# Input projection of a hybrid layer: weights stationary, 512 tokens a row, seven products for eight, and head data through DRAM

## The chip, the cores and the metric

One NeuronCore of a Trainium2 chip runs the whole layer. The metric is the device time of one launch in microseconds; three timed runs of the kernel before gave 1645.48, 1645.70 and 1645.99 (median 1645.7). Engines are named as the profile names them: PE (TensorE), PEld (its weight loads), DVE (VectorE), ACT (ScalarE), POOL (GpSimd), and SP, whose queue issues most DMAs.

## The reference, cut to what matters

The layer takes 1024 latent tokens and 256 context tokens of width 1024. It normalises and modulates them, and multiplies them with one wide matrix:

```
IN_WIDTHS = (512, 512, 512, 512, 512, 512, 512, 512, 16, 1024, 1024)
rq, rk, rv, rg, mq, mk, mv, mo, mg, bg_ret, bg_ml = (h @ w for w in jnp.split(w_in, offsets, axis=-1))
rq = apply_rope(to_heads(rq, 4), cos, sin); rk = apply_rope(to_heads(rk, 4) * 128 ** -0.5, cos, sin)
ret_x = retention(rq, rk, rv) forward + backward, chunks of 128, from the context's final state
ml_x = mlstm(mq, mk, mv, mg) forward + backward, in the same way
merged = sigmoid(bg_ret) * (y_ret @ w_ret_up) + sigmoid(bg_ml) * (y_ml @ w_ml_up)
x = x + g1 * (merged @ w_out)
x = x + g2 * swiglu(modulate(rms_norm(x)), w_ffn_in, w_ffn_out); out = rms_norm(x)
```

Four retention heads and four mLSTM heads of 128 columns each need keys, values, queries and an output gate (rg or mo). The context needs keys and values only. The queries and keys of retention are rotated by position: their two halves are mixed with cosines and sines. The 16 columns mg are the gates of the mLSTM. All is in float32.

## The kernel before, in words

**Products in parts.** A float32 operand is split into two float32r parts, hi (a rounded copy, made on ACT) and lo (the rest, made on DVE), and a product is three matmuls, hi x hi, hi x lo and lo x hi (`mm3`, L89 to L95). Weights come in by DMA as `raw`, 512 columns at a time, and are split into `whi` and `wlo` (`load_w_half`, L73 to L83).

**Projection.** Modulated tokens lie feature-major (`xh` for latents, `ch` for context). For a chunk of 128 tokens, `project` (L447) keeps a 128 x 128 piece of the tokens stationary and moves a row of 256 weight columns past it (272 with the gate columns, for the first block), 24 matmuls to one PSUM tile. `kv_tile` (L459) does this for the key and the value of a head for ten chunks, of which the first two are context; `qg_tile` (L470) for query and gate for eight. The result is token-major, as the scans want it; `rope` (L438) rotates it on DVE and POOL. The first four chunks are computed while the modulation is still being made (`first_tiles`, L348).

**Heads and scans.** Loop L787 goes through heads u = 1 to 7. After each chunk's tile it calls `tick` (L726), which advances what runs beside the projection by one slot: the scan of head u - 1 (`scan`, L481), the gate recurrence (`gates`, L626, under head 1), and the modulation of the later stages (`ada2`, L702, from head 2 on). The scan reads keys, values, queries and gates from SBUF; it transposes queries and keys on PE (`stage_a`, L536), forms scores (`stage_b`), outputs (`stage_c`), states (`decay` on POOL at L497, `advance` with PE at L511), and writes y to DRAM (`put_y`). The gate recurrence goes chunk by chunk: transposes, two scans of 128 per direction on DVE (L656, L658), and columns back by PE.

**Lift and merge.** Retention outputs are lifted with `w_ret_up` (`up_mm`, L808) and parked in DRAM. Then come the gate columns bg: eight blocks of 256 output columns by 1024 inputs. The first is computed plainly (`plain_block`, L239: 96 matmuls of 512 columns); seven are computed by Winograd's form (`winograd_block`, L249: seven products of 512 inputs x 128 columns x 512 tokens in place of eight, 84 matmuls). For that form `seven` (L203) builds seven weight factors from four quarters, and `factors_of_parts` (L872) four token factors `t1` to `t4`. Seven additions per block, on DVE, put the products together.

**Later stages.** Output projection with `mm3` (rows of 512), second norm, FFN (two plain blocks, then 20 blocks of seven products), FFN output and final norm.

**Order.** Each engine works through its instructions in a fixed order. That order is laid out when the kernel is built, by an estimate of readiness, and isn't the order of the text. Waits between engines are semaphores. PSUM has eight tiles of 512 columns: four `mm`, four `sc`.

## Time and profile before

| what | value |
|---|---|
| median of three runs | 1645.7 us |
| span of the profiled execution, first to last instruction | 1643.1 us |
| around the span, against the median | 2.6 us |
| PE busy | 1604.8 us, 98% |
| PEld busy | 1395.8 us, 85% |
| DVE busy | 1005.4 us, 61% |
| ACT busy | 631.2 us, 38% |
| POOL busy | 423.6 us, 26% |
| DMA | 199.13 MB, mean 121 GB/s |

The profile lists the span of its execution and no device time of its own; what lies around the span is therefore taken against the median. The head stage runs from about 130 to 600 us, lift and merge to about 866, the output projection and second norm to about 990, the FFN to 1360, its output to the end. A matmul's busy time overlaps its neighbours', so the pace of PE is read from the distance of starts in a timeline, not from the mean time of one.

### The profile page before, as it was taken

Reading aid. Unit: us, or ns where it says so; the run is one execution under the profiler, and the core shown is the slowest. Engines: PE = TensorE matmul, PEld = TensorE weight load, DVE = VectorE, ACT = ScalarE, POOL = GpSimd, SP = SyncE. Lnnn points to the kernel's source line nnn. Section 1 sums busy time; section 2 is a strip of 40 time slices with the busy share of each in tenths; the row PEclk is TensorE's granted clock in tenths of the full one; section 3 lists DMA queues with packets and bytes.
Section 4 is the critical chain, followed back from the end, with each engine's and each line's share of the span. In section 5 each row is a group of like instructions: output and inputs, shape, how many; then the busy total and the mean of one; then the engine's idle time right before and its main releaser. Section 6 shows DMA issues by size and latency. Waiting matters only on the chain.

```text
span 1643.1 us, 25962 instructions
## 1 busy us (share of the span) xinstructions
PE 1604.8 (98%) x9326; PEld 1395.8 (85%) x9326; DVE 1005.4 (61%) x2223; ACT 631.2 (38%) x1512; POOL 423.6 (26%) x593
## 2 busy tenths in 40 slices
PE   7998999999999999999999999999999999999997
PEld 2798999999999998888877777888888888887887
DVE  5768555644645445678875777667677666536233
ACT  4555332333435355443343453323333334423230
POOL 1546244332322422233330225111111111001001
PEclk9999999999999999999999999999999999999998
DMA  9211223332432244444457412222222224735531
GB/s 328 103 62 35 73 84 104 100 101 91 136 104 91 71 149 135 161 173 161 142 183 252 130 56 71 90 96 85 96 84 83 92 88 168 268 108 179 162 103 52
DMA packets 114033, 199.13 MB, mean 121 GB/s; under 512 B 13104, under 2 KB 24048, under 8 KB 113904
## 3 DMA queue, kind: packets, MB, share of 16 engines
q1 hardware_dynamic: 112032, 195.38, 36.1%
q10 hardware_dynamic: 1872, 2.10, 0.4%
q8 instruction: 73, 1.20, 0.3%
q14 instruction: 56, 0.46, 0.1%
HBM read 160.66 MB, written 36.77 MB: 120 GB/s over the span
## 4 chain that ended last, share of the span: by engine, by line
PE 79%; DVE 7%; POOL 5%; issue 5%; DMA 2%; ACT 1%; SPq 0%; DVEq 0%; POOLq 0%; ACTq 0%
PE mm L95 9%; PE mm L93 9%; PE mm L94 9%; PE mm L1127 5%; PE mm L1129 5%; PE sc L229 5%; PE sc L230 5%; PE sc L231 5%; PE mm L1128 5%; PE mm L229 5%; PE mm L231 5%; PE mm L230 5%; PE sc L511 2%; PE sc L328 1%; POOL hid L995 1%
## 5 line engine op out<-in xcount | busy, mean ns | idle before, releaser
L93 PE MATMUL mm<-whi,A 128*128 128x256 f32 (+1 forms) x992 | 289.8, 292 | 0.9 <-DVE gtok L468 0.9
L95 PE MATMUL mm<-whi,A 128*128 128x256 f32 (+1 forms) x992 | 281.7, 284 | 0.2 <-DVE A L316 0.2
L94 PE MATMUL mm<-wlo,A 128*128 128x256 f32 (+1 forms) x992 | 281.3, 284 | 0.0
L174 DVE TENSOR_TENSOR wlo<-raw,whi 128x512 fp32r<-128x512 f32 x178 | 132.1, 762 | 114.8 <-ACT whi L173 114.6
L93 PEld LDWEIGHTS mm<-whi,A 128*128 128x128 f32 x992 | 190.3, 192 | 1.4 <-DVE gtok L468 1.1
L173 ACT CAST whi<-raw 128x512 fp32r<-128x512 f32 x178 | 106.2, 619 | 221.6 <-PE mm L1128 79.8
L95 PEld LDWEIGHTS mm<-whi,A 128*128 128x128 f32 x992 | 190.2, 192 | 0.5 <-DVE A L316 0.4
L94 PEld LDWEIGHTS mm<-wlo,A 128*128 128x128 f32 x992 | 190.6, 192 | 0.0
L995 POOL TENSOR_TENSOR hid<-hid,sg 128x512 f32<-128x512 f32 x44 | 84.8, 1931 | 329.0 <-DVE hid L255 294.0
L229 PE MATMUL mm<-A,whi 128*128 128x512 f32 x320 | 124.7, 390 | 2.4 <-DVE sg L255 1.7
L230 PE MATMUL mm<-A,whi 128*128 128x512 f32 x320 | 125.2, 391 | 1.0 <-DVE A L316 1.0
L231 PE MATMUL mm<-A,wlo 128*128 128x512 f32 x320 | 125.0, 391 | 0.0
L82 DVE TENSOR_TENSOR wlo<-raw,whi 128x512 fp32r<-128x512 f32 (+1 forms) x112 | 76.4, 708 | 53.6 <-ACT whi L81 53.6
L173 ACT CAST whi<-stg 128x512 fp32r<-128x512 f32 x108 | 61.9, 618 | 106.7 <-PE sc L230 62.2
L81 ACT CAST whi<-raw 128x512 fp32r<-128x512 f32 (+1 forms) x112 | 65.3, 619 | 41.1 <-PE mm L94 13.9
L497 POOL TENSOR_SCALAR vs<-v,colq 128x129 f32<-128x129 f32 x72 | 48.0, 676 | 127.6 <-PE sc L511 127.6
L229 PE MATMUL sc<-A,whi 128*128 128x512 f32 x208 | 80.9, 389 | 0.0
L230 PE MATMUL sc<-A,whi 128*128 128x512 f32 x208 | 80.9, 389 | 0.0
L231 PE MATMUL sc<-A,wlo 128*128 128x512 f32 x208 | 80.9, 389 | 0.0
L174 DVE TENSOR_TENSOR wlo<-stg,whi 128x512 fp32r<-128x512 f32 x108 | 80.0, 779 | 0.7 <-ACT whi L173 0.7
L1127 PE MATMUL mm<-A,whi 128*128 128x512 f32 (+1 forms) x204 | 77.8, 382 | 0.0
L1129 PE MATMUL mm<-A,wlo 128*128 128x512 f32 (+1 forms) x204 | 77.8, 381 | 0.0
(350 smaller groups left out, 4057.1 us busy)
## 6 DMA issues: line engine op xcount, KB each, us to landing
raw<-wffn SPq DMA_DIRECT2D x88, 256.0 KB
raw<-wfo SPq DMA_DIRECT2D x88, 256.0 KB
raw<-wada SPq DMA_DIRECT2D x64, 256.0 KB
raw<-win SPq DMA_DIRECT2D x60, 256.0 KB
hid_d<-hid SPq DMA_DIRECT2D x44, 256.0 KB
hraw<-hid_d SPq DMA_DIRECT2D x40, 256.0 KB
araw<-wada SPq DMA_DIRECT2D x32, 256.0 KB
bc<-rows_d SPq DMA_DIRECT2D x64, 128.0 KB
```

What stands on the lines that cost most here:

```text
L93: nc.tensor.matmul(ps, lhsT=lh, rhs=rh, start=i == 0, stop=False)
L94: nc.tensor.matmul(ps, lhsT=lh, rhs=rl, start=False, stop=False)
L95: nc.tensor.matmul(ps, lhsT=ll, rhs=rh, start=False, stop=i == n - 1)
L173: nc.scalar.copy(hi, x)
L174: nc.vector.tensor_tensor(out=lo, in0=x, in1=hi.bitcast(F32), op=ALU.subtract)
L229: nc.tensor.matmul(ps, lhsT=w[0][:, c], rhs=x[0][:, k, :], start=start and k == 0, stop=False)
L230: nc.tensor.matmul(ps, lhsT=w[0][:, c], rhs=x[1][:, k, :], start=False, stop=False)
L231: nc.tensor.matmul(ps, lhsT=w[1][:, c], rhs=x[0][:, k, :], start=False, stop=stop and k == 3)
L995: nc.gpsimd.tensor_tensor(out=c, in0=c, in1=sgs[f, hf], op=ALU.mult)
L1127: nc.tensor.matmul(ps, lhsT=w[0][:, c], rhs=h[0][:, t], start=kt == 0, stop=False)
L1128: nc.tensor.matmul(ps, lhsT=w[0][:, c], rhs=h[1][:, t], start=False, stop=False)
L1129: nc.tensor.matmul(ps, lhsT=w[1][:, c], rhs=h[0][:, t], start=False, stop=kt == 2 * NG - 1)
```

## The change

- **Projection.** Weights are stationary, and rows of 512 tokens move. Output is feature-major: 128 columns of a head by 512 tokens. Head 0 is computed plainly; heads 1 to 7 by seven products, two blocks a head (key and value, query and gate), with the form that the gate blocks and the FFN have. The token factors t1 to t4 are built once, right after the second half of the latents is modulated, and serve the heads and all eight gate blocks.
- **The form itself.** `winograd_block` now lets four products of a block run on in one PSUM tile (`chain`) and two in another (`third`); ACT copies three intermediate states (`snap`) and the last result, DVE does three additions. `run_blocks` places a block's last two products behind the first of the next. The FFN uses it too. PSUM's four `mm` tiles are now two `ch` and two `ts`. One of the weight sums goes to POOL.
- **Context.** Keys and values of the context are 48 matmuls of 256 columns a head (`context_kv`). For heads 1 to 7 the context's parts are read back from DRAM (`context_stream`) for each head.
- **Head data.** Keys, values and gates are transposed to token-major on PE (`store_tokens`), queries and keys stay feature-major as well, and all are written to DRAM. `scan` of head u - 2 loads them back chunk by chunk; its transposes of queries and keys are gone. Rotation gets the swapped halves by two DMAs (`rotated`).
- **Gates.** The 16 gate columns are 32 matmuls of 512 columns and 16 of 256 (`gate_products`), and the recurrence is done for all ten chunks at once, with scans of up to 1280.
- **Lift and merge.** The gate blocks follow the heads directly and beside them run the last two scans; their sigmoids go to DRAM. The lift comes last, for both branches, and its results are multiplied and added as they come.

```diff
+    def mm_ps(tag=None):
+        if tag is None:
+            seq[1] ^= 1
+            tag = ("ch", "ts")[seq[1]]
+        return psum.tile([P, 512], F32, tag=tag, bufs=2, name=nm(tag))
...
+    class Factors:
...
+        def make(self, r):
+            def tt(o, x, y, op, eng=nc.vector):
+                eng.tensor_tensor(out=o, in0=x, in1=y, op=op)
+                return parts_of(o)
+            yield parts_of(r["a11"])
+            s1 = stage()
+            yield tt(s1, r["a21"], r["a22"], ALU.add)
+            s2 = wp.tile([P, 512], F32, tag="s2", bufs=1, name=nm("s2"))
+            yield tt(s2, s1, r["a11"], ALU.subtract)
+            yield parts_of(r["a12"])
+            yield tt(stage(), r["a11"], r["a21"], ALU.subtract, nc.gpsimd)
+            yield tt(stage(), r["a12"], s2, ALU.subtract)
+            yield parts_of(r["a22"])
+            if self.a21:
+                yield parts_of(r["a21"])
...
+    def prod(ps, w, x, start, stop, cont=False):
         for k in range(4):
             c = slice(k * P, (k + 1) * P)
-            nc.tensor.matmul(ps, lhsT=w[0][:, c], rhs=x[0][:, k, :], start=start and k == 0, stop=False)
-            nc.tensor.matmul(ps, lhsT=w[0][:, c], rhs=x[1][:, k, :], start=False, stop=False)
-            nc.tensor.matmul(ps, lhsT=w[1][:, c], rhs=x[0][:, k, :], start=False, stop=stop and k == 3)
+            for i, (wp_, xp) in enumerate(((0, 0), (0, 1), (1, 0))):
+                nc.tensor.matmul(ps, lhsT=w[wp_][:, c], rhs=x[xp][k], start=start and k == i == 0,
+                                 stop=cont or (stop and k == 3 and i == 2), skip_group_check=cont)
...
+    def winograd_block(w, x, t, done, new, snaps, tail=None):
         b11, b21, b12, b22 = x
         t1, t2, t3, t4 = t
+        def put(f, hf, p, v):
+            c = new()
+            if v is None:
+                nc.scalar.copy(c, p)
+            else:
+                nc.vector.tensor_tensor(out=c, in0=p, in1=v, op=ALU.add)
+            done(f, hf, c)
+        def snap(i):
+            o = snaps(i)
+            nc.scalar.copy(o, chain)
             return o
+        chain = mm_ps("ch")
+        prod(chain, w[0], b11, True, True)
+        p1 = snap(1)
+        yield
+        third = mm_ps("ts")
+        prod(third, w[1], t1, True, True)
+        yield
+        prod(chain, w[2], t2, False, True, True)
+        u2 = snap(2)
+        yield
+        second = mm_ps("ts")
+        prod(second, w[3], b21, True, True)
+        put(0, 0, second, p1)
+        yield
+        prod(chain, w[4], t3, False, True, True)
+        put(1, 1, third, snap(3))
+        if tail is not None:
+            tail()
+        yield
+        prod(third, w[5], b22, False, True, True)
+        put(0, 1, third, u2)
+        yield
+        prod(chain, w[6], t4, False, True, True)
+        put(1, 0, chain, None)
+        yield
...
+    def run_blocks(blocks, tick=lambda: None):
+        blocks = list(blocks)
+        blocks[0][0].load()
+        late = ()
+        for i, (w, first, products) in enumerate(blocks):
+            first()
+            w.need(5)
+            run = products()
+            next(run)
+            tick()
+            for _ in late:
+                tick()
+            w.need()
+            if i + 1 < len(blocks):
+                blocks[i + 1][0].load()
+            for _ in range(4):
+                next(run)
+                tick()
+            late = run
+        for _ in late:
+            tick()
...
+    def store_tokens(c, dst):
+        pt_ = sc_ps()
+        for i in range(4):
+            nc.tensor.transpose(pt_[:, i * P:(i + 1) * P], c[:, i * P:(i + 1) * P], ident)
+        o = wt()
+        nc.scalar.copy(o, pt_)
+        nc.sync.dma_start(dst, o.rearrange("p (n c) -> p n c", n=4))
+    def head_done(u, part):
+        def rotated(c, hf, scale):
+            sw = wt()
+            nc.sync.dma_start(sw[0:64], c[64:P])
+            nc.sync.dma_start(sw[64:P], c[0:64])
+            t = slice(hf * 512, hf * 512 + 512)
+            o = wt()
+            nc.gpsimd.tensor_tensor(out=sw, in0=sw, in1=sinT[:, t], op=ALU.mult)
+            if scale is None:
+                nc.vector.tensor_tensor(out=o, in0=c, in1=cosT[:, t], op=ALU.mult)
+                nc.vector.tensor_tensor(out=o, in0=o, in1=sw, op=ALU.add)
+            else:
+                nc.vector.scalar_tensor_tensor(out=o, in0=c, scalar=scale, in1=cosT[:, t], op0=ALU.mult, op1=ALU.mult)
+                nc.vector.scalar_tensor_tensor(out=o, in0=sw, scalar=scale, in1=o, op0=ALU.mult, op1=ALU.add)
+            return o
+        def done(f, hf, c):
+            n0 = slice(2 + 4 * hf, 6 + 4 * hf)
+            t = slice(hf * 512, hf * 512 + 512)
+            if part == 0 and f == 0:
+                o = rotated(c, hf, None) if u < H else c
+                nc.sync.dma_start(qk_d[u][:, 1, t], o)
+                store_tokens(o, kv_d[u][:, n0, 0, :])
+            elif part == 0:
+                store_tokens(c, kv_d[u][:, n0, 1, :])
+            elif f == 0:
+                if u < H:
+                    c = rotated(c, hf, QSCALE)
+                else:
+                    nc.scalar.activation(c, c, AF.Copy, scale=QSCALE)
+                nc.sync.dma_start(qk_d[u][:, 0, t], c)
+            elif u < H:
+                nc.sync.dma_start(g_d[u].rearrange("p n c -> p (n c)")[:, t], c)
+            else:
+                store_tokens(c, g_d[u][:, 4 * hf:4 * hf + 4, :])
+        return done
...
+    def context_kv(u, w, parts):
+        pk, pv = sc_ps(), sc_ps()
+        for kt in range(KT):
+            hi, lo = parts(kt)
+            for f, ps in enumerate((pk, pv)):
+                wh, wl = (t[:, kt % 4 * P:(kt % 4 + 1) * P] for t in w(2 * (kt // 4) + f))
+                o = ps[:, :CTX]
+                nc.tensor.matmul(o, lhsT=wh, rhs=hi, start=kt == 0, stop=False)
+                nc.tensor.matmul(o, lhsT=wh, rhs=lo, start=False, stop=False)
+                nc.tensor.matmul(o, lhsT=wl, rhs=hi, start=False, stop=kt == KT - 1)
+        c = wt()
+        nc.scalar.copy(c[:, :CTX], pk[:, :CTX])
+        nc.scalar.copy(c[:, CTX:], pv[:, :CTX])
+        pt_ = sc_ps()
+        for n in range(2):
+            for f in range(2):
+                nc.tensor.transpose(pt_[:, (2 * n + f) * P:(2 * n + f + 1) * P], c[:, f * CTX + n * P:f * CTX + (n + 1) * P], ident)
+        o = wt()
+        nc.scalar.copy(o, pt_)
+        nc.sync.dma_start(kv_d[u][:, 0:2], o.rearrange("p (n f c) -> p n f c", n=2, f=2))
+    def context_stream():
+        last = {}
+        def parts(kt):
+            if kt % 2 == 0:
+                for i in range(2):
+                    last[i] = wt(F32R)
+                    nc.sync.dma_start(last[i].bitcast(F32), ctx_d[i, kt // 2])
+            c = slice(kt % 2 * CTX, (kt % 2 + 1) * CTX)
+            return last[0][:, c], last[1][:, c]
+        return parts
...
+    def gate_products(t0, n, part):
+        ps = sc_ps()[:, :n]
+        for kt in range(KT):
+            for i in range(2):
+                nc.tensor.matmul(ps, lhsT=wgt[kt // 4][:, kt % 4, :], rhs=part(i, kt), start=kt == i == 0,
+                                 stop=i == 1 and kt == KT - 1)
+        e = st.tile([P, 512], F32, tag="araw", bufs=10, name=nm("e"))[:, :n]
+        nc.scalar.copy(e, ps)
+        nc.sync.dma_start(e_d[:, t0:t0 + n], e)
...
+    for k in range(4):
+        x11, x21, x12, x22 = x_raw[0][k], x_raw[0][4 + k], x_raw[1][k], x_raw[1][4 + k]
+        d1, d2 = wt(), wt()
+        nc.vector.tensor_tensor(out=d1, in0=x12, in1=x11, op=ALU.subtract)
+        nc.vector.tensor_tensor(out=d2, in0=x22, in1=d1, op=ALU.subtract)
+        d3 = wt()
+        nc.vector.tensor_tensor(out=d3, in0=x22, in1=x12, op=ALU.subtract)
+        d4 = wt()
+        nc.vector.tensor_tensor(out=d4, in0=x21, in1=d2, op=ALU.subtract)
+        for t, i, d in ((t1, 1, d1), (t2, 2, d2), (t3, 3, d3)):
+            for s in range(2):
+                t[s].append(t_tile(i, s, k))
+            split(t[0][k], t[1][k], d)
+        split(t4[0][k], t4[1][k], d4)
+    t_all = (t1, t2, t3, t4)
...
+        for d, spans in ((0, (slice(0, NT),)), (1, (slice(0, CTX), slice(CTX, NT)))):
+            r = slice(32 * d, 32 * d + H)
+            st_ = 1 if d == 0 else -1
+            for i, sp in enumerate(spans):
+                v = lambda t: t[r, sp][:, ::st_]
+                nc.vector.tensor_tensor_scan(out=v(bb), data0=v(rm), data1=v(gf), initial=0.0, op0=ALU.mult, op1=ALU.add)
+                nc.vector.tensor_tensor_scan(out=v(m), data0=v(gf), data1=v(gi), initial=m[r, 0:1] if i else 0.0,
+                                             op0=ALU.add, op1=ALU.max)
+            yield
...
-    def project(w, n, ncols):
-        ps = mm_ps()[:, :ncols]
-        pairs = []
-        for kt in range(KT):
-            hi, lo = w[kt // 4]
-            pairs.append((tok(n, kt), (hi[:, kt % 4, :], lo[:, kt % 4, :])))
-        mm3(ps, pairs)
-        return ps
...
+        def load(d, n):
+            t = bt([P, 2 * P + 1], "kv", 6)
+            nc.sync.dma_start(t[:, :2 * P], kv_d[u][:, n].rearrange("p f c -> p (f c)"))
+            if not ret:
+                nc.gpsimd.memset(t[:, 2 * P:], 1.0)
+            kv[d, n] = t[:, :P], t[:, P:P + W]
...
+        def load_qk(j):
+            qk[j] = bt([P, 2, P], "qk", 2)
+            nc.sync.dma_start(qk[j], qk_d[u][:, :, j * P:(j + 1) * P])
...
+    def beside(gen, rate=1.0):
+        side.append([gen, rate, 0.0])
...
+    def kv_tail(u, w):
+        return lambda: context_kv(u, lambda i: w[(0, 7, 3, 6)[i]], context_stream())
+    def bg_done(blk):
+        def done(f, hf, c):
+            nc.scalar.activation(c, c, AF.Sigmoid)
+            nc.sync.dma_start(bg_d[blk, f, hf], c)
+        return done
+    def head_blocks():
+        def head(u, part):
+            w = Factors(a["win"][2 * u + part], part == 0)
+            def first():
+                if part == 1:
+                    return
+                if u == 1:
+                    beside(gates(), 0.75)
+                if u == 2:
+                    drain()
+                    es_g.close()
+                    open_scans()
+                    beside(ada2())
+                if u >= 2:
+                    beside(scan(u - 2), 1.3)
+            return w, first, lambda: winograd_block(w, b_all, t_all, head_done(u, part), wt, snap_tile,
+                                                    kv_tail(u, w) if part == 0 else None)
+        def gate(blk):
+            w = Factors(a["wbg"][blk])
+            def first():
+                if blk in (0, 2):
+                    beside(scan(2 * H - 2 + blk // 2), 1.3)
+                if blk == 5:
+                    load_y_ret()
+            return w, first, lambda: winograd_block(w, b_all, t_all, bg_done(blk), wt, snap_tile)
+        for u in range(1, 2 * H):
+            for part in range(2):
+                yield head(u, part)
+        for blk in range(8):
+            yield gate(blk)
...
+        up_ps = {}
+        for br, y in enumerate((y_ret, y_ml)):
+            w = load_w_half(a["wup"][i, br])
+            for hf in range(2):
+                for f in range(2):
+                    c = slice(f * P, (f + 1) * P)
+                    ps = mm_ps() if br == 0 else sc_ps()
+                    mm3(ps, [((w[k][0][:, c], w[k][1][:, c]), y[hf][k]) for k in range(4)])
+                    sg = wt()
+                    nc.sync.dma_start(sg, bg_d[4 * br + i, f, hf])
+                    up_ps[br, f, hf] = m = t_tile(3, f, 2 * hf + br, F32)
+                    nc.vector.tensor_tensor(out=m, in0=ps, in1=sg, op=ALU.mult)
+                    if br == 1:
+                        nc.gpsimd.tensor_tensor(out=m, in0=m, in1=up_ps[0, f, hf], op=ALU.add)
+                        split(mh[hf][0][:, 2 * i + f, :], mh[hf][1][:, 2 * i + f, :], m)
```

## Rows read from the trace of the kernel before

**Rows 1.** The page, busy times: us busy, share of the span, instructions.
```profile
PE 1604.8 (98%) x9326; PEld 1395.8 (85%) x9326; DVE 1005.4 (61%) x2223; ACT 631.2 (38%) x1512; POOL 423.6 (26%) x593
```
**Rows 2.** Busy time by stretch: length, each engine's busy us (instructions), clock, DMA share.
```profile
120.00:200.00 80.00, 73.69 (x600) 70.61 (x599) 57.95 (x222) 35.95 (x134) 38.51 (x122) 0.98 0.18 55
200.00:593.00 393.00, 392.91 (x3343) 392.72 (x3342) 208.11 (x703) 148.27 (x548) 139.33 (x246) 1.00 0.31 96
...
840.00:880.00 40.00, 36.63 (x154) 29.49 (x153) 28.38 (x43) 19.94 (x36) 6.13 (x5) 0.96 0.65 215
...
1040.00:1360.00 320.00, 320.00 (x1414) 264.96 (x1413) 221.28 (x307) 100.62 (x171) 52.79 (x34) 1.00 0.26 87
```
**Rows 3.** Chain of waits in order of time: start us, us, what.
```profile
128.97 0.54 DVE bm L656
...
663.05 3.01 DMA bg_d<-t
...
860.19 2.40 DVE A L174 x3
```
**Rows 4.** Timeline of PE, two stretches: start us, us, engine, line, out<-in, shape.
```profile
88.58 0.29 PE L95 MATMUL mm<-whi,A 128*128 128x272 f32 x1
...
91.23 0.29 PE L95 MATMUL mm<-whi,A 128*128 128x272 f32 x1
...
304.03 0.29 PE L95 MATMUL mm<-whi,A 128*128 128x256 f32 x1
...
306.55 0.28 PE L95 MATMUL mm<-whi,A 128*128 128x256 f32 x1
...
307.79 0.60 PE L607 MATMUL sc<-cpack,q 128*128 128x128 f32 x4
...
308.34 0.28 PE L94 MATMUL mm<-wlo,A 128*128 128x256 f32 x1
```
**Rows 5.** Groups by line and shape on PE: count, busy us, mean ns, idle before.
```profile
L93 PE MATMUL mm<-whi,A 128*128 128x256 f32 x960 | 280.5, 292 | 0.9 <-DVE gtok L468 0.9
...
L93 PE MATMUL mm<-whi,chi 128*128 128x256 f32 x112 | 31.8, 284 | 0.0
...
L93 PE MATMUL mm<-whi,A 128*128 128x272 f32 x32 | 9.2, 288 | 0.0
```
**Rows 6.** Groups by line and shape on DVE.
```profile
L82 DVE TENSOR_TENSOR wlo<-raw,whi 128x512 fp32r<-128x512 f32 x108 | 73.5, 708 | 53.6 <-ACT whi L81 53.6
...
L255 DVE TENSOR_TENSOR cp<-mm,cp 128x512 f32<-128x512 f32 x42 | 28.9, 688 | 20.2 <-PE mm L231 19.0
...
L658 DVE TENSOR_TENSOR_SCAN bm<-gr,mprev 4x128 f32<-4x128 f32 x20 | 9.7, 485 | 0.0
```
**Rows 7.** Timeline of all engines in the FFN, 1104 to 1107 us.
```profile
1104.66 2.38 DVE L174 TENSOR_TENSOR wlo<-raw,whi 128x512 fp32r<-128x512 f32 x2
...
1104.82 1.66 POOL L995 TENSOR_TENSOR hid<-hid,sg 128x512 f32<-128x512 f32 x1 [21.50 <-DVE hid L255]
...
1106.94 0.37 SPq L188 DMA_DIRECT2D raw<-wffn  x1
```
**Rows 8.** Timeline of PE in the output projection, 909 to 914 us.
```profile
908.99 0.96 PE L132 MATMUL sc<-ones,acc 128*128 128x1 f32 x8
...
909.81 0.48 PE L94 MATMUL mm<-A,whi 128*128 128x512 f32 x1
...
913.66 1.12 PE L145 MATMUL sc<-stg,ones 128*128 128x512 f32 x2
```

More of the change, by code (lines that the diff above doesn't have):

```diff
@@ L225, in prod, with plain_quads, __init__, load @@
-    def prod(ps, w, x, start, stop):
+    def plain_quads(src):
+        r = raw_quads(src)
+        return {k: parts_of(r[k]) for k in ("a11", "a21", "a12", "a22")}
+    class Factors:
+        def __init__(self, src, a21=False):
+            self.src, self.a21, self.made = src, a21, []
+        def load(self):
+            self.gen = self.make(raw_quads(self.src))
+        def make(self, r):
[13 more added lines that the diff above has]
+                yield parts_of(r["a21"])
+        def need(self, n=8):
+            while len(self.made) < n:
+                f = next(self.gen, None)
+                if f is None:
+                    break
+                self.made.append(f)
+        def __getitem__(self, i):
+            return self.made[i]
@@ new lines, in context_stream @@
+    def context_stream():
[8 more added lines that the diff above has]
+        return parts
+    QK = ("a11", "a21", "a12", "a22")
+    done_kv, done_qg = head_done(0, 0), head_done(0, 1)
+    for f in range(2):
+        c = wt()
+        nc.scalar.copy(c, first_ps[f])
+        done_kv(f, 0, c)
@@ new lines, in body, with load_y_ret @@
+    es_y = ExitStack()
+    y_ret = [[], []]
+    def load_y_ret():
+        drain()
+        es_b.close()
+        py_ = held["py"] = pool(es_y, "py", side="right")
+        for hf in range(2):
+            for k in range(4):
+                y_ret[hf].append(tuple(py_.tile([P, 512], F32R, name=nm("yr")) for _ in range(2)))
+                load_split(y_d[k, hf], *y_ret[hf][k])
+    run_blocks(head_blocks(), tick)
+    nc.vector.scalar_tensor_tensor(out=a2, in0=mod2[:, 16:24], scalar=1.0, in1=gains[:, 1, :], op0=ALU.add, op1=ALU.mult)
```

872 lines of the change are left out of this document (349 added, 523 removed).

## The prediction

> **What bounds the kernel now.** I read four views, in this order. First the page's busy times: TensorE (PE) is busy 1604.8 us of a span of 1643.1 [rows 1], so nothing is gained but by giving PE less to do or by closing its few gaps. Second the busy times by stage, to see where the gaps lie [rows 2]: in the stage of the heads (200 to 593) PE has none, with VectorE (DVE) busy 208 us of 393 and GpSimd (POOL) 139; gaps stand at 120 to 200 (80 less 73.69, so 6.3 us) and at 840 to 880 (3.4 us). Third the chain of waits, for what fills these gaps [rows 3]: at 129 us the scans of the gate recurrence (bm, L656), at 860 us the splits of the merged tokens (A, L174) just ahead of the output projection. Fourth PE's timeline, for its pace. A busy time of one matmul does not give it, since matmuls overlap; the distance of starts does. With 272 columns there are 21 starts in 2.65 us, 0.126 us each; with 256 columns 21 in 2.52 us, 0.120; four transposes and one 256-column matmul take 0.55 us, so 0.11 for a transpose [rows 4]. With 512 columns, 1414 records touch a stretch of 320 us [rows 2], two of them its edges: 0.2266 each.
>
> So the span is the number of PE's matmuls times their pace, and some 40 us of gaps at start, end and seams. A sum of differences in matmuls is a sum in time as long as the other engines deliver.
>
> **The change part by part.** The sum is made against the profiled execution, 1643.1 us of span; the timed runs have their median 2.6 above it, and I keep that 2.6.
>
> *Projection.* Before: 240 matmuls of 272 columns and 3216 of 256 (the groups of 960, 112 and 32 in [rows 5], once for each of the three lines of mm3, and the smaller ones by the loops): 240 x 0.126 + 3216 x 0.120 = 416.1 us. After, by the code: head 0 has 192 matmuls of 512 columns and 32 for the gate columns; heads 1 to 7 have two blocks of 84; that is 1400 x 0.2266 = 317.2 us; the context adds 400 of 256 columns, 48.0 us. Difference -50.9. About 20 us of it come from the wide rows (1536 of them by 2 x 0.120 less 0.2266), the rest from seven products in place of eight, less the gate columns.
>
> The Trainium skill, "TensorE: Matmul & The Clock Gate", section "Back-to-back issue gap", gives N / 2.4 + 2.5 ns for a matmul of N columns. By it 256 columns take 0.109 us and 512 take 0.216, and the difference would be -33, not -50.9. The rows show 0.120 and 0.2266, so I go by the rows.
>
> *Gate blocks.* The first of the eight was plain, 96 matmuls, and is now one of seven products, 84: -2.7 us.
>
> *Transposes.* Gone are 128 of queries and keys in the scans and 20 of the gates; added are 20 in each of four retention heads and 28 in each of four mLSTM heads, 192. Net 44 x 0.11 = +4.8 us. The other matmuls of the scans, the FFN and the lift stay in number.
>
> PE's work together: -48.8.
>
> *Gaps that go.* The gate recurrence of ten steps becomes a few long scans under head 1: -6.3. The merge now ends with the lift, one half of the tokens before the other, so the splits ahead of the output projection are covered: -3.4. Together with the work -58.5.
>
> *DVE in the heads.* A head took PE 432 x 0.120 + some 14.5 for its scan = 66.3 us; the stretch of 393 us holds 5.9 heads, with DVE at 35.1 us and POOL at 23.5 a head [rows 2]. New on DVE per head: 7 more splits (15 for 8) and 6 sums of weights at 0.708 us, 6 additions from PSUM at 0.688 [rows 6]: 13.3. Rotation moves from 32 small operations to 8 large ones and I count it even. That makes 48.4 us of DVE in a head whose PE work falls to 168 x 0.2266 + 48 x 0.12 + 15.4 = 59.3: from 53% to 82%. POOL goes to about 25 us. Below 59.3 on both, so the throughput holds; but a busy DVE answers late, and PE has 12 x 0.2266 = 2.7 us of cover for the copy and the addition that must lie between products five and six. Bounds: 0, if the order leaves slack; and if no DVE operation ran beside one of POOL, 48.4 + 25 - 59.3 = 14 us a head, 113 for the seven heads and the gate blocks that carry the last scans (as eight heads). I take 1.5 a head, +12: the split in mm3's blocks kept 0.708 with POOL busy a third of the time [rows 2, 6], so most overlaps cost little.
>
> *Gates.* A scan of 128 took 0.485 us [rows 6]. One of 1280 takes between that and 4.9; the two longest exceed a product's 2.7 us by 2.2 each: +4 (0 to 12).
>
> *Entry of the seven products.* 16 differences and 16 splits of tokens, 32 x 0.708 = 22.7, and seven operations for the first factors, 5.0, against 112 x 0.2266 = 25.4 us of PE work for the second half of head 0. Short by 2.3; if they start after the 16 operations that scale those tokens, by another 11.3. I take +5 (0 to 15).
>
> *Round trips.* Rotation now sends the halves past each other by DMA: addition 0.69, two issues at 0.37, DMA 3.01, POOL 1.66, DVE 0.71 [rows 3, 6, 7], 6.8 us from the product to a transpose on PE. Eight such calls and 32 plain ones of about 1.0 (an estimate from the addition) come to 86 us if PE stood still for each; the streamed context adds 28 pairs of loads, each 3.01 against 12 x 0.12 = 1.4 us of products, 44 us. But PE's order is not that of the text: in the output projection the sum of squares (L132) and the broadcast (L145) are two neighbouring calls, and PE runs the other half's products between them [rows 8]. I take +3 of 0 to 130. SP has some 80 issues a head x 0.37 = 30 of 59 us.
>
> *Start and lift.* x comes in twice as many DMAs (8 more issues, 3 us of SP, mostly behind the wait for bytes), and 16 splits of the mLSTM outputs stand ahead of the second half of the lift, covered by 10.9 us of products: +2 (0 to 8).
>
> *FFN.* Same matmuls; four of seven additions leave DVE. PE had no gap, so 0 (0 to +10 if four PSUM banks in place of eight bind).
>
> Sum: -58.5 + 12 + 4 + 5 + 3 + 2 = -32.5. Span 1610.6, time **1613**.
>
> **Rivals.**
> A. All new waits are hidden, as in the heads before, where DVE's 53% left PE no gap: -58.5 + 2, time 1589. For it: every new step has a product to hide behind. Against it: 82% on DVE.
> B. Slower by exclusion. DVE and POOL keep each other out of SBUF. The row for it: a pair of splits took 2.38 us beside one POOL multiplication of 1.66 [rows 7], where two at 0.708 are 1.42. Before, 35.1 + 23.5 = 58.6 us fitted in a head of 66.3 even so; after, 73.4 does not fit in 59.3. If four fifths of POOL's 25 us fall on DVE, a head gets 48.4 + 20 - 59.3 = 9.1 us longer: 8 x 9.1 = 73, less 58.5, plus 14 for the other terms, time 1674. It decides from about 16.5 of the 25 us, where the head's loss is 5.6 us and the gain is gone. Against it: POOL's small operations in the heads left the split at 0.708.
> The Trainium skill, "SBUF — State Buffer", section "SBUF: two separate sides", calls the pair of ports that DVE and GpSimd share an exclusive lock, held for a whole instruction. By that rule the case for B is the full one; row 7 agrees for an operation with two inputs, the mean in row 6 doesn't for the rest.
> C. Slower by waits behind DMAs: if PE stands for half of the 130 us above, 65 in place of 3, time 1675. For it: the order is fixed before the run, and loads, stores and shifts share one queue. Against it: rows 8.
> D. The wide rows give nothing, a 512-column matmul of the projection taking 2 x 0.120: +19, time 1632. Against it: the FFN's pace in [rows 2].
>
> **How the numbers follow.** A: 0.22 (1588 to 1603). Forecast: 0.44 (1603 to 1626). D: 0.05. Something between forecast and no change: 0.08. B: 0.11. C: 0.10. Range 1594 to 1648: it leaves out about 0.08 below, and about 0.13 of B and C above. A change within 0.2% (3.3 us) can't be told from none. Faster: 0.22 + 0.44 + 0.05, 0.06 of the between and 0.02 of weak forms of B and C, 0.79; within 0.2%: 0.04; slower: 0.17.
>
> **What would show it.** Right: 2072 + matmuls of 512 columns at 0.2266 in the stage of projection and gate blocks; a head of about 60 us; PE's gaps in it under 2 us; no gap of 6 us for the gates; the FFN as before. The DVE term is right if DVE is busy some 80% there. B shows as DVE splits well over 1 us in the heads; C as gaps on PE that end with a transpose or with a context load. The prediction is wrong if PE's gaps in the heads add up to over 50 us, or if none exist at all.

## The result, and the profile after

The changed kernel takes 1724.8 us (median of 4 runs, 1719.1 to 1726.7) against 1645.9 for the kernel before, run on the same chip: a ratio of 1.0471, with a 95% interval of 1.0454 to 1.0488. It is 79 us slower; the forecast was 1613 and its range ended at 1648. The profiled execution has a span of 1723.2 us and belongs to a time of 1725.0.

The page of the changed kernel: TensorE (PE) as in [rows 1], the DMA queue, and the chain that ended last.

```profile
PE 1607.6 (93%) x7702; PEld 1300.6 (75%) x7702; DVE 1008.2 (59%) x1986; ACT 690.9 (40%) x1355; POOL 434.2 (25%) x504
...
q1 hardware_dynamic: 186640, 265.06, 49.6%
...
PE 59%; DVE 13%; DMA 12%; issue 4%; POOL 3%; ACT 3%; SPq 1%; DVEq 0%; POOLq 0%; ACTq 0%
```

PE's busy time is the same to 3 us, but it is 93% of the span where it was 98%: the sum of starts times paces fell and the gaps grew. I count a gap as the distance between two starts on PE less the pace of the first matmul (0.227 us for 512 columns, 0.120 for 256, 0.11 for smaller ones; 0.43 for the modulation's 64 of 512 columns in plain float32). By that count PE's work went from 1586.2 to 1538.1 us, -48.1, and its gaps from 39.0 to 165.2, +126.2. Together +78; PE's first start lies 1.6 us later.

Busy time by stretch of the changed kernel, with the columns of [rows 2]: entry and gates, heads, end of heads and gate blocks, the lift, the output projection, and a stretch of the FFN.

```profile
120.00:210.00 90.00, 65.49 (x281) 49.26 (x280) 70.83 (x104) 33.33 (x63) 15.04 (x16) 0.81 0.36 106
210.00:590.00 380.00, 337.50 (x1874) 280.41 (x1873) 243.51 (x598) 144.35 (x354) 135.34 (x194) 0.98 0.71 217
590.00:840.00 250.00, 235.20 (x1220) 197.13 (x1220) 165.00 (x414) 140.91 (x305) 80.17 (x151) 0.99 0.61 183
840.00:935.00 95.00, 95.00 (x414) 77.23 (x413) 44.28 (x68) 23.03 (x39) 19.07 (x14) 1.00 0.56 178
935.00:1100.00 165.00, 159.75 (x691) 128.46 (x690) 114.43 (x192) 72.72 (x119) 48.17 (x25) 0.99 0.37 120
...
1120.00:1440.00 320.00, 319.52 (x1401) 262.02 (x1400) 167.70 (x218) 127.46 (x221) 76.87 (x50) 1.00 0.28 86
```

Read the first column after the length. The lift and the FFN are full, as before. The entry has 24.5 us in which PE is not busy at all, the heads 42.5 of 380 where [rows 2] had 0.1 of 393. DVE is at 64% in the heads, so it has time left; the DMA engines' share went from 0.31 to 0.71. The granted clock is 0.81 in the entry and 0.98 in the heads: behind the gaps, 163 matmuls start while it is at the lower of its two levels (1.2 for 2.4 GHz), at about twice the distance. That is 21 of the 165 us; before the change it was 25 matmuls and 3 of the 39.

Who PE waited for in the heads and gate blocks, 210 to 790 us of the changed kernel (total us, times, longest):

```profile
PE sc L915 <- DVE o L910: 11.2, 11, 2.6
PE sc L509 <- DVE wt L524: 8.2, 4, 5.4
PE sc L866 <- DMA qk<-qk_d: 7.8, 10, 1.7
PE sc L559 <- DMA wt<-ctx_d: 7.1, 5, 2.0
PE sc L509 <- DVE wt L281: 5.9, 6, 1.6
PE sc L820 <- POOL vs L806: 4.8, 5, 2.1
PE sc L560 <- DMA wt<-ctx_d: 3.7, 7, 1.2
```

Every waiting line is a small one: transposes of outputs (L915) and of stored tokens (L509), scores (L866), context (L559, L560), state updates (L820). The products (L251) hardly appear. The longest of these waits, in the changed kernel's chain of waits (start, us, what):

```profile
228.38 0.23 SPq L517
228.62 0.04 issue
228.66 5.36 DMA wt<-wt
...
234.18 1.27 POOL wt L521
235.47 1.20 DVE wt L524
```

This is the rotation: halves swapped by DMA (5.36 us, where I had 3.01 from [rows 3]), GpSimd, DVE, and at 236.72 the transposes. PE stood from 231.3 on, because those transposes come next in its order. The same on PE's timeline at 402 us, with what ended the idle time in brackets: scores whose queries and keys are late (1.73 us), in the middle of a product (L251). Five of its twelve matmuls run ahead of the wait, the other seven behind it.

```profile
399.62 1.32 PE L251 MATMUL ts<-t,fw 128*128 128x512 f32 x5
402.66 0.46 PE L866 MATMUL sc<-qk 128*128 128x128 f32 x2 [1.73 <-DMA qk<-qk_d]
402.95 0.60 PE L509 MATMUL sc<-cpack,wt 128*128 128x128 f32 x4
403.39 0.39 PE L820 MATMUL sc<-vs,kv 128*128 128x128 f32 x2
...
404.43 0.48 PE L251 MATMUL ts<-t,fw 128*128 128x512 f32 x1
...
407.44 0.47 PE L251 MATMUL ts<-t,fw 128*128 128x512 f32 x1
409.47 0.66 PE L866 MATMUL sc<-qk 128*128 128x128 f32 x2 [1.56 <-DMA qk<-qk_d]
409.78 2.48 PE L251 MATMUL ts<-t,fw 128*128 128x512 f32 x5
```

That is the rule here. From 210 to 790 us PE stands 54 times for at least 0.25 us before a small instruction (any but the products' matmuls), 54.8 us in all. In 46 of these stands, 44.3 us, a product is under way, and its next matmul waits for no semaphore of its own: PE could have gone on with it, but its order has the small instruction first.

### The profile page after: what moved, and what is told of

It is laid out like the page before. It is cut to its first block, busy times and chain, and to the rows that moved or that the text cites. A ratio compares the mean times of both kernels' runs of the same rounds, so it can differ in the third digit from the quotient of the medians.

```text
span 1723.2 us, 23184 instructions
## 1 busy us (share of the span) xinstructions
PE 1607.6 (93%) x7702; PEld 1300.6 (75%) x7702; DVE 1008.2 (59%) x1986; ACT 690.9 (40%) x1355; POOL 434.2 (25%) x504
## 4 chain that ended last, share of the span: by engine, by line
PE 59%; DVE 13%; DMA 12%; issue 4%; POOL 3%; ACT 3%; SPq 1%; DVEq 0%; POOLq 0%; ACTq 0%
PE ch L251 15%; PE ts L251 13%; DMA qk<-qk_d 3%; DMA wt<-ctx_d 3%; PE ch L1253 2%; PE ch L1254 2%; PE ch L1252 2%; PE ts L1252 2%; PE ts L1254 2%; PE ts L1253 2%; DMA raw<-wffn 2%; DVE fw L183 2%; DMA kv<-kv_d 2%; PE ch L104 1%; PE ch L103 1%
## 5 line engine op out<-in xcount | busy, mean ns | idle before, releaser
L251 PE MATMUL ts<-A,fw 128*128 128x512 f32 x1176 | 300.8, 400 | 6.4 <-ACT A L386 2.3
L183 DVE TENSOR_TENSOR fw<-raw,fw 128x512 fp32r<-128x512 f32 x282 | 198.3, 707 | 179.5 <-ACT fw L182 179.1
L251 PE MATMUL ch<-A,fw 128*128 128x512 f32 x1176 | 296.6, 395 | 0.0
L251 PEld LDWEIGHTS ts<-A,fw 128*128 128x128 f32 x1176 | 221.2, 192 | 61.2 <-DVE A L388 4.6
L251 PE MATMUL ch<-t,fw 128*128 128x512 f32 x1008 | 256.9, 399 | 8.1 <-ACT u L286 3.4
L182 ACT CAST fw<-raw 128x512 fp32r<-128x512 f32 x282 | 172.4, 621 | 206.3 <-PE ch L1254 86.5
L251 PEld LDWEIGHTS ch<-A,fw 128*128 128x128 f32 x1176 | 220.2, 189 | 45.1 <-ACT wt L286 0.9
L251 PEld LDWEIGHTS ch<-t,fw 128*128 128x128 f32 x1008 | 188.9, 191 | 48.9 <-ACT t L182 4.6
L183 DVE TENSOR_TENSOR fw<-stg,fw 128x512 fp32r<-128x512 f32 x126 | 96.6, 767 | 85.3 <-ACT fw L182 85.0
L251 PE MATMUL ts<-t,fw 128*128 128x512 f32 x504 | 136.4, 405 | 7.1 <-ACT t L182 6.0
L251 PEld LDWEIGHTS ts<-t,fw 128*128 128x128 f32 x504 | 94.4, 191 | 28.0 <-ACT t L182 8.0
L954 DVE SCALAR_TENSOR_TENSOR acc<-stg,silu_c,acc 128x256 f32<-128x256 f32 x112 | 60.2, 538 | 19.2 <-DMA stg<-wada 17.9
L820 PE MATMUL sc<-vs,kv 128*128 128x128 f32 (+1 forms) x288 | 52.6, 286 | 7.9 <-POOL vs L806 4.8
L820 PEld LDWEIGHTS sc<-vs,kv 128*128 128x128 f32 x288 | 44.6, 194 | 13.9 <-POOL vs L806 6.9
```

The costliest lines, as they stand in the source:

```text
L182: nc.scalar.copy(hi, x)
L183: nc.vector.tensor_tensor(out=lo, in0=x, in1=hi.bitcast(F32), op=ALU.subtract)
L251: nc.tensor.matmul(ps, lhsT=w[wp_][:, c], rhs=x[xp][k], start=start and k == i == 0, stop=cont or (stop and k == 3 and i == 2), skip_group ...
L820: nc.tensor.matmul(ps, lhsT=kv[d, n][0], rhs=vsd.pop((d, n)), start=True, stop=True)
L954: nc.vector.scalar_tensor_tensor(out=acc, in0=r2, scalar=s, in1=acc, op0=ALU.mult, op1=ALU.add)
```

## The experiments

Theory 1: PE executes an order planned ahead, and stands where a small instruction is placed closer behind its data than the data is on the chip (trip of a DMA, then an operation of another engine). Rivals: VectorE's amount of work, the one DMA queue, the wt buffers, the seven products themselves. Four runs of the changed kernel spread over 7.5 us, so a single time says little below 8. The gaps of each run show where the time lies, but each experiment has one run and one trace, so a difference of gaps below about 8 us says little either. The columns count 168 of the products' matmuls (L251) each, two blocks, from the first one, at 63.6 us in the changed kernel. The first 144 belong to head 0. So column 0 is the end of head 0 with the first 24 matmuls of head 1, column 1 the rest of head 1 with the first 24 of head 2, and so on; the last three are gate blocks. The recorded expectations call column 0 head 1 and column 1 head 2, one too high. Line numbers differ by a few between runs: L915, L917 and L923 are the same transposes.

```
                   head 0     1     2     3     4     5     6     7 | gate blocks    sum    time
after               12.8  31.5  16.5  13.2  13.1  10.6  14.0  14.4  5.9  3.8  0.4  136.2  1725.0
e1_shift_unread      8.1  25.1  11.5  12.3  12.0  13.1  12.3  14.3  7.0  3.9  1.6  121.2  1711.9
e2_ctx_unread       11.4  25.7  23.9  15.3  11.1   8.5  13.1  10.1  7.1  6.2  0.4  132.8  1718.8
e3_scan_unread      11.0  33.1  21.9  10.3   9.9   8.3  12.8  12.9  4.3  3.7  1.0  129.2  1718.1
e4_all_unread        8.1  24.2  11.6  13.5   9.0   5.8   9.2   9.9  4.1  3.6  1.3  100.3  1687.7
e9_no_lo             7.0  29.7  17.9  11.7  10.7   7.7  13.6  13.8  6.4  5.3  0.9  124.7  1705.2
e10_all_no_lo        5.6  21.9   8.8  11.4   3.3  12.1   6.8   9.5  3.7  3.2  0.5   86.8  1667.0
e16_no_gates        10.6  18.6  10.4  15.0  13.1   7.1  10.4  13.2  5.1  3.5  0.5  107.5  1694.6
e17_no_transposes    5.5  30.6  21.7  12.2   7.4  10.4  11.0   9.5  7.1  4.1  0.5  120.0  1689.3
e12_no_scans        12.5  30.5   6.5  11.7   9.8   2.8   5.6   4.3 -0.1 -0.1 -0.1   83.4  1568.2
e18_bare             5.8  17.5   9.8   9.5   6.9   1.4   3.9   3.7 -0.1 -0.1 -0.1   58.2  1521.1
e7_later            10.3  30.6  16.7  19.2   5.4  10.5  10.7   9.5  6.1  8.2  0.9  128.1  1717.4
e13_later150        16.6  28.2  25.2  21.1  18.6  22.4  16.9  24.9 13.2 13.6 -0.1  200.6  1789.8
e11_other_plan      27.7  30.5  24.8  21.3  16.4  20.6  20.7  20.9 15.1 13.4  3.6  215.0  1794.1
```

**Transfers that nobody waits for.**

```diff
 # e1: rotation
-            nc.sync.dma_start(sw[0:64], c[64:P])    # and the other half
-            nc.gpsimd.tensor_tensor(out=sw, in0=sw, in1=sinT[:, t], op=ALU.mult)
+            nc.sync.dma_start(unread[0:64], c[64:P])
+            nc.gpsimd.tensor_tensor(out=sw, in0=c, in1=sinT[:, t], op=ALU.mult)
 # e2: context_stream
-            return last[0][:, c], last[1][:, c]
+            return xh[0][0][:, kt, 0:CTX], xh[0][1][:, kt, 0:CTX]
 # e3: scan
-            kv[d, n] = t[:, :P], t[:, P:P + W]
+            one = dt_all.rearrange("p h t -> p (h t)")
+            kv[d, n] = one[:, :P], one[:, P:P + W]
...
+            qk[j] = dt_all[:, 0:2, :]
```

> Left out: the swap of the two halves in the rotation of keys and queries (the swap's two transfers still run, into scratch that nothing reads; GpSimd multiplies the unswapped rows). If PE's stands come from the trip of the swapped halves (theory: PE, in its fixed order, stands behind data that is on its way through a DMA), the four retention heads lose a chain of one DMA each product, and the 92 us that PE stands between 210 and 780 us fall by 15 to 25 us. If vector engines' work or the buffers set the stands, or the DMA engines' load does (the transfers are all still there), by under 5 us.

> Changed: the context rows of heads 1 to 7 are projected from resident tokens; the 8 transfers a head that brought the context back from DRAM still run and nothing reads them. If PE stands behind data on its way, the 15.6 us in which it waited for these transfers go, and what stood behind them in PE's order moves up: 12 to 25 us of the 92. If it is load, engines or buffers: under 5 us, since every transfer is still there.

> Changed: the scans' keys, values and queries come from a resident table; the 19 and 8 transfers a head that load them still run and nothing reads them. If PE stands behind data on its way: 11.7 us (scores) and 13.3 us (state updates, whose factor GpSimd scales from the loaded values) go, 20 to 35 us of the 92 with what stands behind them. If it is load, engines or buffers: under 8 us.

> The three edits at once (halves not swapped, context rows from resident tokens, the scans' keys, values and queries from a resident table); all transfers still run. If PE in its fixed order stands behind transfers, 55 to 90 of the 92 us between 210 and 780 us go, and the kernel takes 1635 to 1670 us. If the engines' own work, the rotation of buffers or the load of the DMA engines sets the stands, 1700 us or more.

Measured: gaps 15.0, 3.4 and 7.0 us less, and 35.9 less together, where the three alone add to 25.4; the time of e4 falls by 37. The 92 us of the expectations are columns 2 to 7 and the gate blocks but the last pair; there it is 5 us less, 4 more, 7 less, and 25 less together. So each alone gives the rivals' answer, or nearly, and the three together lie between the two answers: transfers are 36 of the 136 us, not the most of it. Stands can move to the next late instruction (in e2 column 2 went from 16.5 to 23.9, about the scatter). What PE waits for in e4, 210 to 760 us, is for the most part DVE, the outputs' norm (L912), the additions (L281) and the rotation's sum (L524):

```profile
PE sc L917 <- DVE o L912: 12.1, 13, 2.8
PE sc L509 <- DVE wt L281: 7.8, 7, 2.2
PE sc L509 <- DVE wt L524: 4.8, 4, 2.1
PE sc L509 <- ACT wt L279: 4.5, 3, 3.0
PE sc L960 <- DVE acc L956: 4.2, 3, 1.8
```

**DVE's work.**

```diff
 # parts_of, e9; e10 is e4 with it
-        split(hi, lo, x)
-        return hi, lo
+        nc.scalar.copy(hi, x)
+        return hi, hi
```

> Left out: VectorE's subtraction that makes the low part of each split weight factor in the projection, the gate blocks and the FFN (the high part is used twice; ScalarE's copies and all matmuls stay). In a head VectorE loses some 15 operations of 0.71 us, 11 of its 31 us. Theory that VectorE's lateness sets the pace of the heads (what remained when the three transfers were unread was put down to it almost alone): PE's 92 us between 210 and 780 us fall by 30 us or more. Theory that PE's planned order stands behind transfers first, and VectorE is late because it too waits for them: by under 15 us.

> The three edits that leave transfers unread and the low parts left out, at once. If the stands come from transfers and from VectorE, the two added: of the 92 us under 25 are left and the time is 1625 to 1655 us. If the plan itself leaves gaps on PE (its buffers and its order, whatever the durations on the chip): more than 45 us are left and the time stays over 1670 us.

Measured: DVE's busy time from 210 to 690 us falls from 310 to 255; the gaps by 11.5 us (4 of the 92), and by 8 more behind the lift. (DVE's 31 us a head in the expectation should be some 47.) So DVE's amount of work is not the pace of the heads. With the transfers unread too, 58.8 of the 92 remain. That is the second answer to e10 (more than 45), though the time of 1667.0 us is 3 under its 1670: most of the gaps lie in neither of the two.

**The queue and the buffers.**

```diff
 # e5: four stores (transposed tokens, context rows, outputs, gates)
-        nc.sync.dma_start(dst, o.rearrange("p (n c) -> p n c", n=4))
+        nc.scalar.dma_start(dst, o.rearrange("p (n c) -> p n c", n=4))
 # e8
-        return pw.tile([P, 512], dt, tag="wt", bufs=5, name=nm("wt"))
+        return pw.tile([P, 512], dt, tag="wt", bufs=6, name=nm("wt"))
```

> The whole computation. The stores of transposed tokens, context rows, head outputs and gates are issued by ScalarE, which writes most of what they store, in place of SyncE. Theory of the one queue (in the heads SyncE stood 31 us for head outputs, 23 us for token tiles, 12 for context rows and 16 for gates, with all loads queued behind): the loads come earlier and PE's 92 us between 210 and 780 us fall by 15 us or more. Theory that PE's planned order stands behind the trips themselves and behind VectorE: under 6 us either way, or a loss where an issue on ScalarE holds up the next copy.

> The whole computation; the wt tiles, through which products, rotations, transposed tokens and the context rows pass, have 6 buffers in place of 5 (room from one buffer less of loaded keys and values, of scaled values and of the start's raw tiles, and the squares' unused output put into PSUM). If the rotation of wt is what releases late (each is held some 3 to 5 us by its transfer), PE's 92 us in the heads fall by 12 to 30 us. If not, within 6 us.

Measured: e5 1731.1 us with 140.7 us of gaps, e8 1724.9 with 134.8. Neither shortens the gaps beyond the scatter. In e8 the room came from one buffer less of loaded keys and values, of scaled values and of the start's raw tiles, so a gain that these took back isn't excluded.

**The order alone.**

```diff
 # e7 (60, four kinds of instructions) and e13 (150, all small kinds), as here
+        with tc.high_priority(offset=-60):
             for i in range(4):
                 nc.tensor.transpose(pt_[:, i * P:(i + 1) * P], c[:, i * P:(i + 1) * P], ident)
 # e11
-    with tile.TileContext(nc) as tc:
+    with tile.TileContext(nc, schedule_with_timeline_sim=True) as tc:
```

> The whole computation; only the planned order on PE differs: transposes of tokens and outputs, state updates and scores are given a place about one and a half products later (their priority is lowered by 60 places). If PE stands because the plan puts these before their data is there on the chip, the 92 us between 210 and 780 us fall by 20 to 50 us. If the chain of buffers or the engines set the pace, the gaps only move to other instructions, and the time stays within 8 us or grows.

> The whole computation, the same instructions: the order of each engine is planned with the planner's other timing, its simulation of the timeline. If PE's stands are a matter of how the planned order fits the chip's own durations, the time moves by over 10 us (either way) and the list of instructions that PE waits in changes; if they are set by chains of data and buffers that any order has, it stays within 8 us.

> The whole computation, the same instructions; in the plan, PE's transposes, scan matmuls, context matmuls and modulation columns have their priority lowered by 150 places (about four products), where e7_later lowered four of these kinds by 60 and gained 7 us. If the order's distance to the data is what counts, 15 to 45 us less than the kernel after. If the chains through the buffers bind first, within 10 us of e7_later.

Measured: 8.1 us of gaps less, 78.8 more, and 64.4 more, with the same instructions. Two other orders cost tens of us, some 20 in each by matmuls at the lower clock. No order tried gives tens of us back: e7, forecast at 20 to 50 of the 92, gave 5 there, the rivals' answer. Its stands inside products halved (44.3 to 21.7 us), while the products' own waits rose from 1.1 to 8.7. e13 misses its forecast by its sign: put off that far, the outputs' transposes wait even longer. That the scan's chain ahead of them was put off too is the likely reason, not shown. PE in e13, 64 to 800 us:

```profile
PE sc L923 <- DVE o L917: 42.8, 7, 7.9
PE sc L562 <- DMA wt<-ctx_d: 22.0, 13, 4.0
```

**The entry.** In the changed kernel's chain, DVE runs in one row from 139.5 to 153.7 us while PE gets on by a few matmuls at a time: differences of the tokens (L651 to L656), their splits (L183) and a gate operation between them.

```profile
139.53 0.68 DVE wt L652
140.21 0.60 DVE wt L654
140.81 0.60 DVE wt L656
141.41 1.80 DVE t L183 x3
143.22 0.60 DVE A L183
...
149.84 1.46 DVE g L681
```

```diff
 # e6: first two blocks, e14: first block (there with t4 made in the second block)
+            for f in range(2):
+                prod(ps, w[f and 2], top, True, False)
+                prod(ps, w[f and 3 or 1], bot, False, True)
 # e16
     def gates():
+        nc.gpsimd.memset(colq, 1.0)    # and wold, rows_d
+        yield
+        return
```

> The whole computation; the first two blocks of head 1 are computed with eight plain products each, so that PE has work that needs no t factor while VectorE makes these. PE does 24 more matmuls of 512 columns (+5.4 us). If the 21.6 us of gaps at 118 to 166 us are the wait for the t factors, 12 to 20 of them go: net 6 to 14 us faster than the kernel after, with the clock at full in 120 to 160 us. If they are VectorE's whole queue there (factors, gates, rotations), the gaps move behind 166 us and the net is -3 to +5 us.

> The whole computation; only the first block of head 1 has eight plain products, and the last of the four t factors, whose tiles hold the second half's upper input until then, is made in the second block from the parts. PE does 12 matmuls of 512 columns more (+2.7 us), VectorE 8 subtractions (+5 us). If the entry's gaps are the wait for t factors: 8 to 16 us faster than the kernel after. If they are VectorE's whole queue there, within 4 us.

> Left out: the recurrence of the mLSTM gates (its tables are filled with ones). If VectorE's work for it, beside the t factors and the first weight factors, is what holds PE in heads 1 and 2, their 44 us of gaps fall to 15 to 25, and the time by 18 to 30 us. If the t factors alone hold them, by under 8 us.

Measured: e6 1712.1 us with 119.5 us of gaps, 16.7 less, as its first answer had it. (Its expectation calls it the whole computation; the tiles of one input hold the fourth t factor by then, and its products read that in the input's place. The work is as told.) e14, which does compute everything, has one plain block in place of two and eight subtractions more on DVE: 1725.8 us with 136.0. Column 0 falls to 8.4, and column 1 rises to 32.7. So the t factors are the front of DVE's row, and with them out of PE's way for one block only, the wait moves behind them. There stands the gate recurrence. Without it (e16) 28.7 us of gaps go, but columns 0 and 1 keep 29.2 of their 44.3, where 15 to 25 was forecast; the other 13.6 go behind them, 6 at most in a column. The time falls by 30. Its long scans are no worse than I had priced, 2.8 us for 1280 (bounds 0.485 to 4.9), but three pairs of them and six operations of some 1.5 us stand in one row with factors and rotations. e15_both joined e13 and e14:

> The whole computation; the later places of e13_later150 and the entry of e14_entry at once. If the two causes are apart, their gains add within 6 us; if both are VectorE's one queue, the sum falls short by more.

It took 1783.9 us, 6 less than e13: nothing to read there.

**What is left.**

```diff
 # e12
     def scan(u):
+        for hf in range(2):
+            nc.sync.dma_start(y_d[u, hf], qk_d[u][:, 0, hf * 512:hf * 512 + 512])
+            yield
+        return
 # e17; e18 is e12, e16 and e17 together
-        pt_ = sc_ps()
...
-        nc.sync.dma_start(dst, o.rearrange("p (n c) -> p n c", n=4))
+        nc.sync.dma_start(dst, c.rearrange("p (n c) -> p n c", n=4))
```

> Left out: the scans (state updates, scores, outputs, their loads and the transposes of the outputs; the projection, its rotations, transposes and stores stay, and a copy in DRAM stands for the outputs). PE loses about 29 us of scan matmuls and transposes. If the gaps in the heads are PE's small matmuls planned close behind their data, the gaps between the third block and the merge (123 us) fall under 60 us, what is left being the stored tokens' transposes, the context and the modulation columns. If they belong to the seven products themselves (their weight factors and drains on VectorE and ScalarE), over 85 us are left.

> Left out: PE's transposes of keys, values and output gates before they are stored, with ScalarE's copy behind them (rows of the product are stored as they are). If PE's place for them right behind the product is what costs, the 20 us of gaps that end in them go and some of what follows: 20 to 35 us of gaps less, beside 20 us or so less of PE's own work (46 sets of four). If the late data behind them (rotations, drains) only shows next in the scans' instructions, under 12 us of gaps less.

> Left out together: the gate recurrence, the stored tokens' transposes and the scans. What PE still has in the heads are the seven products, the context rows with their transposes and the modulation columns. If the products themselves run without gaps and PE's small instructions in the planned order are what costs, under 30 us of the 136 us of gaps are left, most of it in head 1. If weight factors and drains hold the products too, over 50 us.

Measured: without scans 52.8 us of gaps less. Of the 123 us from column 1 on, 70.9 are left, between the two answers, 30.5 of them in column 1. From column 5 on (386 us) PE is 95% busy and more, in the last two of these stretches:

```profile
210.00:370.00 160.00, 143.21 (x702) 115.48 (x701) 95.93 (x171) 51.27 (x99) 21.12 (x15) 0.97 0.67 206
370.00:530.00 160.00, 152.33 (x778) 124.04 (x777) 90.27 (x160) 58.67 (x104) 11.12 (x8) 1.00 0.65 198
530.00:690.00 160.00, 159.38 (x706) 131.06 (x705) 83.79 (x121) 81.88 (x142) 7.89 (x7) 1.00 0.46 143
```

Without the stored tokens' transposes 16.2 less, short of 20 to 35. With recurrence, transposes and scans out, 58.2 are left, not under 30, so the strong form of the theory falls: the products wait too. PE in e18, 64 to 640 us:

```profile
PE ts L251 <- DVE wt L281: 12.6, 6, 5.4
PE sc L554 <- DMA wt<-ctx_d: 4.9, 3, 4.1
PE sc L555 <- DMA wt<-ctx_d: 4.6, 8, 1.8
PE ts L251 <- ACT t L182: 3.8, 4, 1.7
PE ch L251 <- DVE t L183: 3.0, 4, 1.9
```

A product waits for its PSUM buffer, which DVE's addition (L281) has still to drain. Gaps of 0.3 us and more make 41 of the 58 us; these waits are most of them. The other 17 are smaller distances, about half of them at the lower clock.

Shown: PE stands inside products that could go on, 44 of the 56 us between 210 and 790 us. By what was left out: scans 53, gate recurrence 29, token transposes 16 us (98 alone, 78 together); across these, late transfers 36. Leaving work out also takes its load off the other engines and the DMA queue, so these sizes are of the work as a whole, not of its place in PE's order. Open: what an order planned with the chip's own durations would give; no run had one. No version that computes the whole layer beats the kernel before.

## Why the prediction was wrong

- *PE's work*, -48.8: right, -48.1. The counts were as worked out (1388 more of 512 columns, 2816 fewer of 256, 240 of 272 gone) and the paces held, 0.227 and 0.120.
- *Round trips*, +3 of 0 to 130: the step that failed; the gaps rose by 126 us. Rival C, which I gave 0.10, had the direction and, with 65 us of waits, half the size, but its cause, the DMAs, holds only a part. I read [rows 8] as PE stepping around late data. It shows only that the order isn't the text's; it is planned ahead, and on the chip PE stands in it with work at hand (44.3 us inside products). The sign that I gave for it, "gaps on PE that end with a transpose or with a context load", is what the waits show. The three kinds of transfers hold 36 us (e4). The scans, whose loads these partly are, hold 53 (e12), and the stored tokens' transposes 16 (e17); hand-offs from DVE, GpSimd and ScalarE to PE had no term in the sum. The 3.01 us that I put in for a swap and for a load is the time of a store (bg_d<-t). In [rows 2] the same scans ran beside heads with no gap, reading keys, values and queries that never left SBUF.
- *DVE in the heads*, +12: the work was right and the mechanism wrong. 243.5 us in 380 of heads that take some 74 us each is 47 us a head (predicted 48.4), but the head grew, so DVE is at 64%, not 82%. Rival B's exclusion exists, but is small. From 200 to 840 us, 142 DVE operations of 128x512 with two inputs in SBUF that met no GpSimd operation took 0.69 us each, 50 that began beside a GpSimd operation with one tensor as input 0.70, and 13 that began beside one with two 1.28, the longest 1.79. One of the 13, the rotation's sum of the chain above, with the GpSimd operation that it met:

```profile
235.40 0.72 POOL L855 TENSOR_TENSOR qs<-qk,dec 128x256 f32<-128x256 f32 x1
235.47 1.20 DVE L524 TENSOR_TENSOR wt<-wt,wt 128x512 f32<-128x512 f32 x1 [4.00 <-POOL wt L521]
```

That makes some 8 us of DVE's time (13 x 0.59), where B had 73 on the whole, so B falls by its size. The Trainium skill, "SBUF — State Buffer", section "SBUF: two separate sides", has an exclusive lock, held for the whole instruction, between a DVE operation with two SBUF inputs and a GpSimd operation that reads SBUF. The trace agrees where the GpSimd operation has two inputs, and not where it has one (0.70 us). A busy DVE cost by answering late, which I named and then priced at 1.5 us a head.
- *Gates* +4, *entry* +5, and the 6.3 us that should go: together -6.3 + 9, against 44.3 us of gaps in columns 0 and 1, of which 15.1 go without the recurrence (e16) and, by the same count, 17.9 with two plain blocks at the entry (e6). I added two costs as if each had DVE to itself; they stand in one row on it.
- *Gaps at the merge*, -3.4, *start and lift*, +2, *FFN*, 0: right to within 3 us. From the first output projection on the kernel takes 787.9 us, where it took 786.8.

## What to carry over

Before moving data out to DRAM and back beside a full engine, count the small instructions on that engine that depend on it, and look up how far behind their data the fixed order puts them; a throughput sum for the other engines says nothing on this. A stretch without a gap before the change shows only that its old hand-offs were covered. Several costs that are each small must be laid in one row where they share an in-order engine.

## What the runs showed that I had not expected

A swap of 64 rows by DMA took from 2.65 to 5.36 us and a load of queries and keys from 2.78 to 4.88 us on the chain, where a store took 3.01 in [rows 3]. The share of the DMA engines doesn't tell them apart: it was 0.71 around that store (655 to 670 us of the kernel before), 0.27 around a swap of 3.43 us (120 to 160 us) and 0.77 around the one of 5.36 (220 to 240 us). VectorE's operations with two inputs in SBUF took 1.28 us in place of 0.69 beside GpSimd operations with two inputs, and 0.70 beside those with one. The same instructions in three planned orders took 1717, 1790 and 1794 us, 1725 in the kernel's own. And removing waits does not add up: three kinds of work left out gave 98 us alone and 78 together; three kinds of unread transfers gave 25 alone and 36 together, though that difference is near the scatter.
